# A softplus as small GpSimd operations, and a regrouped fill, in a delta-net mixer

## The chip, the cores and the metric

The kernel runs on one core of one Trainium2 chip. The metric is the device time of one execution in microseconds (us). The engines are named as the profile names them: PE is TensorE's matmul, PEld its weight load, DVE is VectorE, ACT is ScalarE, POOL is GpSimd, SP is SyncE, which here issues DMAs only.

## The reference

Two layers of a decoder trunk on 256 tokens of width 1024, all in float32. Each layer is: half a SwiGLU feed-forward network (FFN), a token mixer, a cross-attention into 256 memory tokens, half an FFN, each on a normalised input and added to x. In layer 0 the mixer is dilated attention beside a gated linear recurrence. In layer 1 it is a gated DeltaNet with 8 heads of 128, the part that the change is about:

```
qkv, z, a, b = split(h @ w_in)                      # 3*1024, 1024, 8, 8 columns
q, k, v = split(silu(causal_dwconv(qkv, conv_w)))   # q, k normalised per head
beta = sigmoid(b)
g = -exp(a_log) * softplus(a + dt_bias)             # log decay, per token and head
o = gated_delta_rule_chunked(q, k, v, g, beta)
o = rmsnorm(o, o_norm) * silu(z)
x = x + o @ w_out
```

The delta rule takes cumulative sums of g, `decay = exp(gcum_i - gcum_j)` below the diagonal, the matrix `I + strict(beta * k k^T * decay)`, a triangular solve with it, and a recurrence over chunks. Layer 0 has a second, smaller softplus: that of `-lam`, for the recurrence.

## The kernel before, in words

**Layout and weights.** Activations stand transposed, features on the 128 partitions and the 256 tokens along the free dimension. A weight block of 1024 rows and 256 columns is a unit. It comes from memory in halves (`raw`), and each half is split into a high part (ACT, L158) and a low part (DVE, L159), `wt`. A product is then a 512-column matmul (L200) and a 256-column one (L204), a pair. A unit has 16 pairs and yields four times. After every yield comes `tick`, which splits the next half of a weight and runs what is due: `self.after(n, fn)` puts a step n ticks ahead.

**The delta-net mixer (`mixer1`).** It first projects the 128 columns that hold a and b. Then `DN_ORDER` gives four parts. The first is nine units (k0 k1 q0 q1 k2 v0 k3 v1 z0; each covers two heads). The second is `back` for the head pairs 0 and 1 with the units after the bar (v3 z1 v2 q2) as fill between its steps. The third is the unit q3 alone. The fourth is `back` for the pairs 2 and 3 with z2 z3 K2 K3 as fill (K are keys of the cross-attention). Each projected unit goes from PSUM (`psw`, three buffers) through an add on ACT and DVE (L270, L271), a convolution (L1071, L1074) and a SiLU.

**The decays.** `AB` sets when, in ticks after the a/b projection, `betas`, `decays`, `decay_rows` and the four loads of e are due. `betas` transposes a and b (L1032), adds the bias (`ga`, L1035), runs `softplus` (L742 to L752, which calls `log1p_of`, a series in z = e / (e + 2)), and multiplies by -exp(a_log) to get g (L1039). `decays` sums g with two matmuls (L1044, L1045). `decay_rows` transposes the sums and writes them to DRAM through ACT's DMA queue (`gd`, L1058). `decay` copies a mask into e on SP's queue and has GpSimd's queue load `gd` onto it, adding (L1119); ACT takes the exponential (L1125) at the ticks of `EXP`. With e, `matrix` (at `NK`) makes `na` (L1169), which is stored, inverted in blocks of 16 on DVE (L1233, L1235) and loaded again as `tu`. `KST`, `QST` and `VST` hold the ticks of the other steps of keys, queries and values.

**The end of a group.** `back` squares and sums o (L1327), takes a power -1/2 on GpSimd (L341, `ro`), and `gated` multiplies o by it and by silu(z) (L1339). `gated_T` transposes the result (L1348) and writes the input of the output projection, a2, as a high part (ACT, L1349) and a low part (DVE, L1350). For pairs 0 and 1 both are due a few ticks into the unit q3. For pairs 2 and 3 they stand at the end of the part, and the output projection follows. `DN_FILL` holds how many yields of fill come after each step of `back`, then ahead of each `gated_T`; what is left comes last.

**What sets the order.** The program is written in this order, but the framework's planner makes one list of instructions for each engine ahead of the run, by its own estimate of when each input is ready, and may move an instruction past others. On the chip each engine runs its list in order.

```
DN_FILL = ((1, 1, 1, 1, 1, 1, 1, 1, 1, 2, 2, 1), (1, 1, 1, 1, 1, 1, 1, 1, 1, 1, 1, 0, 5, 0))
AB = (3, 5, 8, 10, 11, 12, 12)
```

Of the kernel before, what the change touches and what calls it, by code (L numbers as in the profile page):

```python
# [9 lines left out]
F32 = mybir.dt.float32  # L10
# [4 lines left out]
OP = mybir.AluOpType  # L15
# [3 lines left out]
P = 128  # L19
# [6 lines left out]
NEG = -1e30  # L26

DN_ORDER = ('k0 k1 q0 q1 k2 v0 k3 v1 z0', '01|v3 z1 v2 q2', 'q3', '23|z2 z3 K2 K3')
DN_FILL = ((1, 1, 1, 1, 1, 1, 1, 1, 1, 2, 2, 1), (1, 1, 1, 1, 1, 1, 1, 1, 1, 1, 1, 0, 5, 0))
YB = 5  # L30
EB, QB, VB = (4, 3, 3)
TWICE = 'k0 k1 q0 q1'.split()
MASK = 2
EXP = (16, 17, 22, 23)
KST = (0, 7, 3)
QST = (2, 9, 5)
VST = 10
AB = (3, 5, 8, 10, 11, 12, 12)
NK = (13, 10, 10, 9)
INV = (3, 4, 13, 14)  # L40
NST = 1
COVER = (3, 1)
# [5 lines left out]
LN_TERMS = 8  # L48
# [19 lines left out]
class Net:  # L68
# [363 lines left out]
    def setup(self, ctx):  # L432
        nc, tc, t = self.nc, self.tc, self.t
# [8 lines left out]
        c = self.p_c  # L442
# [7 lines left out]
        nc.vector.memset(self.ones, 1.0)  # L450
        self.mhalf = c.tile([P, 32], F32, name="mhalf")
        nc.vector.memset(self.mhalf, -0.5)
        self.prm = c.tile([P, P], F32, name="prm")
        self.dcw = c.tile([P, P], F32, name="dcw")

# [4 lines left out]
        x = t["x"][0].rearrange("(t p) d -> p t d", p=P)  # L460
# [263 lines left out]

    def log1p_of(self, pool, e, n, name):

        nc = self.nc
        z = pool.tile([P, n], F32, name=name + "z")
        y = pool.tile([P, n], F32, name=name + "y")
        s = pool.tile([P, n], F32, name=name + "s")  # L730
        nc.vector.tensor_scalar(z, e, 2.0, None, op0=OP.add)
        nc.vector.reciprocal(z, z)
        nc.vector.tensor_mul(z, z, e)
        nc.vector.tensor_mul(y, z, z)
        nc.vector.tensor_scalar(s, y, 2.0 / (2 * LN_TERMS + 1), None, op0=OP.mult)
        for i in range(LN_TERMS - 1, 0, -1):
            nc.vector.scalar_tensor_tensor(s, s, 2.0 / (2 * i + 1), y, op0=OP.add, op1=OP.mult)
        nc.vector.scalar_tensor_tensor(s, s, 2.0, z, op0=OP.add, op1=OP.mult)
        return s

    def softplus(self, pool, x, n, name, sign=1.0):

        nc = self.nc
        m = pool.tile([P, n], F32, name=name + "m")
        e = pool.tile([P, n], F32, name=name + "e")
        nc.vector.tensor_scalar(m, x, sign, 0.0, op0=OP.mult, op1=OP.max)
        nc.vector.tensor_scalar(e, x, -1.0, None, op0=OP.mult)
        nc.vector.tensor_tensor(e, e, x, op=OP.min)
        nc.scalar.activation(e, e, AF.Exp)
        s = self.log1p_of(pool, e, n, name)  # L750
        nc.vector.tensor_add(s, s, m)
        return s  # L752

    def attn_consts(self, mp, tmp):
# [246 lines left out]
    def mixer1(self, mid, kT_mem, mem_mov, gnext):  # L1001
        nc, tc, t = self.nc, self.tc, self.t
# [3 lines left out]
        with tc.tile_pool(name="m1", bufs=1, reuse_waits="tile") as mp:  # L1006
# [9 lines left out]
            for ks in (range(4), range(4, 8)):  # L1016
# [6 lines left out]
            beta, nbeta, ga, g, gc, ngc, kd, eg, nb_all, hb_all, rq_all, ro_all = map(small, (  # L1023
                "beta", "nbeta", "ga", "g_dn", "gc", "ngc", "kd", "eg", "nb_all", "hb_all", "rq_all", "ro_all"))
# [4 lines left out]
            def betas():  # L1029
                pt = self.bank("s")  # L1030
                for c in range(2):
                    nc.tensor.transpose(pt[:, 0, tok(c)], ab[:, tok(c)], self.ident)  # L1032
                av = pt[:, 0].rearrange("p (c n) -> p c n", c=2)[:, :, 112:120]
                bv = pt[:, 0].rearrange("p (c n) -> p c n", c=2)[:, :, 120:128]
                nc.vector.tensor_add(ga, av, dtb[:, None, :].to_broadcast([P, 2, 8]))  # L1035
                nc.scalar.activation(beta, bv, AF.Tanh, scale=0.5)
                nc.vector.tensor_scalar(nbeta, beta, -0.5, -0.5, op0=OP.mult, op1=OP.add)
                gs = self.softplus(mp, flat(ga), 16, "dt")
                nc.vector.tensor_mul(g, gs.rearrange("p (a b) -> p a b", a=2),  # L1039
                                     nea[:, None, :].to_broadcast([P, 2, 8]))  # L1040

            def decays():
# [52 lines left out]
            def square(y):  # L1095
                sq = mp.tile([P, 2, S], F32, name="th", bufs=2)
                nc.scalar.activation(sq, y, AF.Square)
                return sq
# [12 lines left out]
            def decay(p, n):  # L1111

                e = four("e", EB)

                def mask():
                    nc.sync.dma_start(e, neg_up[:, None, :].to_broadcast([P, 4, P]))

                def load():
                    nc.gpsimd.dma_start(e, bass.AP(tensor=gd.tensor, offset=gd.offset + 4 * p * P,  # L1119
                                                   ap=[[0, P], [1, 4 * P]]), accum_op=OP.add)  # L1120

                def exp():
                    for j in range(2):
                        for c in range(2):
                            nc.scalar.activation(e[:, 2 * j + c], e[:, 2 * j + c], AF.Exp,  # L1125
                                                 bias=ngc[:, c, 2 * p + j:2 * p + j + 1])
                    st[p]["e"] = e

                self.after(MASK, mask)
                self.after(n, load)  # L1130
                self.after(EXP[p], exp)

# [3 lines left out]
            def key_steps(p, y, n, twice):  # L1136
# [40 lines left out]

                k0, k1, k2 = KST
                self.after(k0, lambda: s.update(sq=square(y)))
# [154 lines left out]
            def gated(p):  # L1334
                o, z = st[p]["o"], st[p].pop("z")
                for j in range(2):
                    for c in range(2):
                        i = 2 * j + c
                        nc.vector.scalar_tensor_tensor(o[:, i], o[:, i], ro_all[:, c, 2 * p + j:2 * p + j + 1],  # L1339
                                                       z[:, c, j * P:j * P + P], op0=OP.mult, op1=OP.mult)  # L1340

            def gated_T(p):
                o = st[p].pop("o")
                hs = slice(2 * p, 2 * p + 2)
                po = self.bank("s")
                for j in range(2):
                    for c in range(2):
                        nc.tensor.transpose(po[:, j, tok(c)], o[:, 2 * j + c], self.ident)  # L1348
                nc.scalar.activation(a2[:, hs, 0], po, AF.Copy, scale=onorm)  # L1349
                nc.vector.scalar_tensor_tensor(a2[:, hs, 1], po, onorm, a2[:, hs, 0].bitcast(F32),  # L1350
                                               op0=OP.mult, op1=OP.subtract)
# [3 lines left out]
            def unit(step):  # L1355
# [16 lines left out]
                if kind == "k":  # L1372
                    yks[c] = y
                    key_steps(c, y, NK[c], twice)
                elif kind == "q":
# [3 lines left out]

            assert AB[0] < AB[1] < AB[2] < min(AB[3:]) and max(AB[3:]) < min(EXP)  # L1380
            self.after(AB[0], betas)
            self.after(AB[1], decays)
            self.after(AB[2], decay_rows)
            for p in range(4):
                decay(p, AB[3 + p])
            for i, part in enumerate(DN_ORDER):
                if i % 2 == 0:
                    for step in part.split():
                        self.run(unit(step))
                    continue  # L1390
                group, bg = part.split("|")
                gens = [back(int(p)) for p in group]
                bg = deque(unit(step) for step in bg.split())
                parts = list(DN_FILL[i // 2])
                if i == 1:
                    self.fill(bg, 2)
                while gens:
                    gens = [g_ for g_ in gens if next(g_, 0) is None]
                    if gens:
                        self.fill(bg, parts.pop(0))  # L1400
                if i == 1:
                    self.fill(bg)
                    for n, p in enumerate(group):
                        self.after(1 + n, lambda p=int(p): gated(p))
                        self.after(4 + n, lambda p=int(p): gated_T(p))
                    continue
                for p in group:
                    gated(int(p))
                for p in group:
                    self.fill(bg, parts.pop(0))  # L1410
                    gated_T(int(p))
                self.fill(bg)
# [64 lines left out]
```

## Time and profile before

| | |
|---|---|
| median of three runs | 1252.36 us (1251.72 to 1255.6) |
| the profiled execution | 1251.99 us, its span 1250.2 us |
| granted clock of PE | 0.998 of full speed |
| busy: PE, PEld | 1236.0 us (99%), 1104.9 us (88%) |
| busy: DVE, ACT, POOL | 929.0 us (74%), 752.0 us (60%), 80.5 us (6%) |
| the delta-net mixer in the trace | from 770 us to some 973 us of the span |

The matmuls are pipelined and their ends are modelled, so a busy PE can hide short gaps. A row of the timeline gives the start, the duration, the engine, the line, the operation, output<-input with their shapes, and the count. A bracket at its end holds the idle time of that engine before it and what ended it. A row of waits names who waited, for whom, how long in total, how often, and the longest. A row of a group ends with the busy time, the mean duration in ns, and the idle time before.

### The profile page before, as it was taken

What the parts mean: (1) busy time and instruction counts of PE and PEld (TensorE: products, weight loads), DVE (VectorE), ACT (ScalarE), POOL (GpSimd) and SP (SyncE); (2) the same over time, 40 slices, a digit from 0 to 9 for tenths busy, and PEclk for the clock granted to TensorE, in tenths of its full rate; (3) what the DMA queues carried; (4) which work ended last, traced back from release to release, by engine and by line L of the source; (5) the groups of instructions that cost most, each with busy time, mean ns of one, the idle gap of its engine ahead of it and who ended that gap; (6) DMA issues with size and microseconds to landing.
All of it is one profiled execution on the core that took longest, in us unless ns stands there. A gap on an engine that the chain in (4) does not pass through costs nothing.

```text
span 1250.2 us, 20300 instructions
## 1 busy us (share of the span) xinstructions
PE 1236.0 (99%) x7702; PEld 1104.9 (88%) x7702; DVE 929.0 (74%) x1590; ACT 752.0 (60%) x1281; POOL 80.5 (6%) x96
## 2 busy tenths in 40 slices
PE   9999999999999999999999999999999999999997
PEld 8888889888998888888888888888898998888887
DVE  6987957788668778766877756989757668777753
ACT  7766545886555665545656544776757465666543
POOL 1000020000101000011000001020001101000000
PEclk9999999999999999999999999999999999999999
DMA  8766676544544566557666566667534535666561
GB/s 272 215 206 197 185 255 185 178 125 152 185 135 154 185 198 184 183 185 231 187 187 195 181 192 204 183 153 193 142 99 135 181 124 169 185 186 194 177 194 60
DMA packets 231019, 222.92 MB, mean 178 GB/s; under 512 B 14969, under 2 KB 228617, under 8 KB 230793
## 3 DMA queue, kind: packets, MB, share of 16 engines
q1 hardware_dynamic: 229448, 217.94, 56.9%
q0 software_dynamic: 1152, 3.15, 1.0%
q8 instruction: 60, 0.98, 0.3%
q10 hardware_dynamic: 320, 0.53, 0.1%
q14 instruction: 39, 0.31, 0.1%
HBM read 215.03 MB, written 5.51 MB: 176 GB/s over the span
## 4 chain that ended last, share of the span: by engine, by line
PE 90%; DVE 5%; ACT 2%; DMA 1%; issue 1%; POOL 1%; ACTq 0%; DVEq 0%; POOLq 0%
PE psw L200 21%; PE pss L200 16%; PE psw L204 11%; PE psf L200 11%; PE pss L204 8%; PE psf L204 5%; PE psw L242 5%; PE psf L242 4%; PE pss L242 3%; PE psw L216 2%; DVE wt L159 1%; PE psw L220 1%; ACT wt L158 1%; PE pss L1268 1%; PE psf L1274 1%
## 5 line engine op out<-in xcount | busy, mean ns | idle before, releaser
L159 DVE TENSOR_TENSOR wt<-raw,wt 128x1024 fp32r<-128x1024 f32 (+1 forms) x409 | 484.9, 1191 | 202.8 <-ACT wt L158 199.6
L158 ACT ACTIVATE wt<-raw 128x1024 fp32r<-128x1024 f32 (+1 forms) x409 | 418.6, 1031 | 172.1 <-PE psw L204 59.4
L200 PE MATMUL psw<-x,wt 128*128 128x512 f32 x864 | 310.6, 396 | 2.1 <-DVE xn L271 1.8
L204 PE MATMUL psw<-x,wt 128*128 128x256 f32 x864 | 224.9, 281 | 0.5 <-DVE wt L159 0.5
L200 PE MATMUL pss<-x,wt 128*128 128x512 f32 x520 | 187.4, 393 | 0.0
L200 PEld LDWEIGHTS psw<-x,wt 128*128 128x128 f32 x864 | 160.6, 188 | 30.1 <-issue 2.1
L204 PEld LDWEIGHTS psw<-x,wt 128*128 128x128 f32 x864 | 162.4, 188 | 9.4 <-DVE wt L159 1.0
L204 PE MATMUL pss<-x,wt 128*128 128x256 f32 x520 | 134.9, 280 | 0.0
L200 PE MATMUL psf<-x,wt 128*128 128x512 f32 x352 | 127.2, 394 | 0.0
L200 PEld LDWEIGHTS pss<-x,wt 128*128 128x128 f32 x520 | 97.7, 188 | 16.9 <-ACT bc L377 0.4
L204 PEld LDWEIGHTS pss<-x,wt 128*128 128x128 f32 x520 | 97.7, 188 | 5.4
L200 PE MATMUL psw<-h,wt 128*128 128x512 f32 x264 | 94.9, 396 | 0.0
L204 PE MATMUL psf<-x,wt 128*128 128x256 f32 x352 | 91.3, 280 | 0.0
L200 PE MATMUL pss<-h,wt 128*128 128x512 f32 x242 | 87.0, 396 | 0.0
L336 POOL TENSOR_TENSOR acc<-acc,sq 128x256 f32<-128x256 f32 x49 | 43.7, 891 | 658.3 <-ACT sq L334 557.3
L200 PEld LDWEIGHTS psf<-x,wt 128*128 128x128 f32 x352 | 66.1, 188 | 11.2
L204 PE MATMUL psw<-h,wt 128*128 128x256 f32 x264 | 72.0, 280 | 0.0
L204 PEld LDWEIGHTS psf<-x,wt 128*128 128x128 f32 x352 | 66.2, 188 | 3.5
L204 PE MATMUL pss<-h,wt 128*128 128x256 f32 x242 | 66.0, 280 | 0.0
L200 PEld LDWEIGHTS psw<-h,wt 128*128 128x128 f32 x264 | 49.6, 188 | 10.8
L200 PE MATMUL psf<-h,wt 128*128 128x512 f32 x154 | 55.4, 397 | 0.0
L200 PEld LDWEIGHTS pss<-h,wt 128*128 128x128 f32 x242 | 45.5, 188 | 9.8
(377 smaller groups left out, 2109.2 us busy)
## 6 DMA issues: line engine op xcount, KB each, us to landing
raw<-in_ffn_w_in_dram SPq DMA_DIRECT2D x175, 512.0 KB, 3.6
raw<-in_ffn_w_out_dram SPq DMA_DIRECT2D x80, 512.0 KB, 3.6
raw<-in_xa_wkv_dram SPq DMA_DIRECT2D x32, 512.0 KB, 3.5
raw<-in_dn_w_in_dram SPq DMA_DIRECT2D x32, 512.0 KB, 4.6
raw<-in_ab_w_in_dram SPq DMA_DIRECT2D x20, 512.0 KB, 3.6
raw<-in_xa_wq_dram SPq DMA_DIRECT2D x16, 512.0 KB, 3.5
raw<-in_xa_wo_dram SPq DMA_DIRECT2D x16, 512.0 KB, 3.4
raw<-in_ffn_w_out_dram SPq DMA_DIRECT2D x16, 256.0 KB, 2.9
```

Source lines behind the costliest of these rows:

```text
L158: nc.scalar.activation(a, r, AF.Copy)
L159: nc.vector.tensor_sub(b, r, a.bitcast(F32))
L200: nc.tensor.matmul(out.rearrange("p a s -> p (a s)"), w[:, 0, cols], mov[:, k].rearrange("p a s -> p (a s)"), start=k == start, stop=k == ...
L204: nc.tensor.matmul(out[:, 0], w[:, 1, cols], mov[:, k, 0], start=False, stop=False)
L216: nc.tensor.matmul(out.rearrange("p a s -> p (a s)"), mov[:, k, 0, tok], w.rearrange("p a s -> p (a s)"), start=k == 0, stop=k == KD - 1)
L220: nc.tensor.matmul(out[:, 0], mov[:, k, 1, tok], w[:, 0], start=False, stop=False)
L242: self.nc.tensor.matmul(out, a[u], b[w], start=first and i == 0, stop=last and i == 2)
L336: (eng or nc.gpsimd).tensor_add(self.acc, self.acc, sq)
L1268: nc.tensor.matmul(py[:, i], na[:, i], tu[:, 0, i], start=True, stop=True)
L1274: nc.tensor.matmul(pp[:, i], yy[:, i], tu[:, 1, i], start=True, stop=True)
```

## The change

The softplus runs on GpSimd instead of VectorE, in both places where it is used; only its exponential stays on ACT. It is written with other operations: the minimum of x and -x as -2 max(x, 0) + x, the reciprocal as a power -1 against a constant tile `mone`, and each step of the series as a multiplication and an addition instead of one fused operation. Before the exponential three operations stand as before; after it, the multiplication by -exp(a_log) included, there are 22 instead of 15. The series has the same terms.

The multiplication that gives g moves to GpSimd as well. The tables AB, KST, NK and EXP shift the steps of the decays and keys. For the head pairs 0 and 1 `gated` comes at ticks 2 and 3 instead of 1 and 2, `gated_T` at 6 and 7 instead of 4 and 5. The second group's fill has 9 yields between the steps of `back` instead of 11, 4 ahead of the first `gated_T` instead of 5, and 3 left for after the second one instead of none.

```diff
-DN_FILL = ((1, 1, 1, 1, 1, 1, 1, 1, 1, 2, 2, 1), (1, 1, 1, 1, 1, 1, 1, 1, 1, 1, 1, 0, 5, 0))
+DN_FILL = ((1, 1, 1, 1, 1, 1, 1, 1, 1, 2, 2, 1), (1, 0, 1, 1, 0, 1, 1, 1, 1, 1, 1, 0, 4, 0))
-EXP = (16, 17, 22, 23)
-KST = (0, 7, 3)
+EXP = (16, 18, 22, 23)
+KST = (0, 7, 5)
-AB = (3, 5, 8, 10, 11, 12, 12)
-NK = (13, 10, 10, 9)
+AB = (2, 7, 9, 10, 10, 11, 11)
+NK = (13, 11, 10, 9)
@@ setup
         nc.vector.memset(self.mhalf, -0.5)
+        self.mone = c.tile([P, 32], F32, name="mone")
+        nc.vector.memset(self.mone, -1.0)
@@ log1p_of
-        nc.vector.tensor_scalar(z, e, 2.0, None, op0=OP.add)
-        nc.vector.reciprocal(z, z)
-        nc.vector.tensor_mul(z, z, e)
-        nc.vector.tensor_mul(y, z, z)
-        nc.vector.tensor_scalar(s, y, 2.0 / (2 * LN_TERMS + 1), None, op0=OP.mult)
-        for i in range(LN_TERMS - 1, 0, -1):
-            nc.vector.scalar_tensor_tensor(s, s, 2.0 / (2 * i + 1), y, op0=OP.add, op1=OP.mult)
-        nc.vector.scalar_tensor_tensor(s, s, 2.0, z, op0=OP.add, op1=OP.mult)
+        eng.tensor_scalar(z, e, 2.0, None, op0=OP.add)
+        eng.tensor_tensor(z, z, self.mone[:, :n], op=OP.pow)
+        eng.tensor_mul(z, z, e)
+        eng.tensor_mul(y, z, z)
+        eng.tensor_scalar(s, y, 2.0 / (2 * LN_TERMS + 1), 2.0 / (2 * LN_TERMS - 1), op0=OP.mult, op1=OP.add)
+        for i in range(LN_TERMS - 2, -1, -1):
+            eng.tensor_mul(s, s, y)
+            eng.tensor_scalar(s, s, 2.0 / (2 * i + 1), None, op0=OP.add)
+        eng.tensor_mul(s, s, z)
@@ softplus
-        nc.vector.tensor_scalar(m, x, sign, 0.0, op0=OP.mult, op1=OP.max)
-        nc.vector.tensor_scalar(e, x, -1.0, None, op0=OP.mult)
-        nc.vector.tensor_tensor(e, e, x, op=OP.min)
+        eng.tensor_scalar(m, x, sign, 0.0, op0=OP.mult, op1=OP.max)
+        eng.tensor_scalar(e, m, -2.0, None, op0=OP.mult)
+        (eng.tensor_add if sign > 0 else eng.tensor_sub)(e, e, x)
         nc.scalar.activation(e, e, AF.Exp)
         s = self.log1p_of(pool, e, n, name)
-        nc.vector.tensor_add(s, s, m)
+        eng.tensor_add(s, s, m)
@@ mixer1
-                nc.vector.tensor_mul(g, gs.rearrange("p (a b) -> p a b", a=2),
+                nc.gpsimd.tensor_mul(g, gs.rearrange("p (a b) -> p a b", a=2),
-                        self.after(1 + n, lambda p=int(p): gated(p))
-                        self.after(4 + n, lambda p=int(p): gated_T(p))
+                        self.after(2 + n, lambda p=int(p): gated(p))
+                        self.after(6 + n, lambda p=int(p): gated_T(p))
```

More of the change, by code (lines that the diff above doesn't have):

```diff
@@ L725, in log1p_of @@
     def log1p_of(self, pool, e, n, name):
-        nc = self.nc
+        eng = self.nc.gpsimd
         z = pool.tile([P, n], F32, name=name + "z")
@@ L743, in softplus @@
         nc = self.nc
+        eng = nc.gpsimd
         m = pool.tile([P, n], F32, name=name + "m")
         e = pool.tile([P, n], F32, name=name + "e")
-        nc.vector.tensor_scalar(m, x, sign, 0.0, op0=OP.mult, op1=OP.max)
-        nc.vector.tensor_scalar(e, x, -1.0, None, op0=OP.mult)
-        nc.vector.tensor_tensor(e, e, x, op=OP.min)
+        eng.tensor_scalar(m, x, sign, 0.0, op0=OP.mult, op1=OP.max)
+        eng.tensor_scalar(e, m, -2.0, None, op0=OP.mult)
+        (eng.tensor_add if sign > 0 else eng.tensor_sub)(e, e, x)
         nc.scalar.activation(e, e, AF.Exp)
         s = self.log1p_of(pool, e, n, name)
-        nc.vector.tensor_add(s, s, m)
+        eng.tensor_add(s, s, m)
         return s
```

## The prediction

> **What bounds the kernel now.** I read the page first, then the waits of TensorE (PE), then stretches of the delta-net mixer.
>
> ```profile
> span 1250.2 us, 20300 instructions
> ...
> PE 1236.0 (99%) x7702; PEld 1104.9 (88%) x7702; DVE 929.0 (74%) x1590; ACT 752.0 (60%) x1281; POOL 80.5 (6%) x96
> ```
>
> PE sets the end: 14.2 us of the span are not PE work, and nothing in the diff takes work from PE. A gain can only come out of stalls of PE. The waits of PE, longest first (total, times, longest, in us):
>
> ```profile
> PE psw L200 <- DVE xn L271: 1.8, 1, 1.8
> PE psf L200 <- DVE a L1350: 1.3, 1, 1.3
> PE psw L491 <- DVE mhalf L452: 1.1, 1, 1.1
> PE pss L1348 <- DVE qk L1339: 1.0, 1, 1.0
> ...
> PE psw L216 <- DVE tm L1233: 0.4, 1, 0.4
> ```
>
> All but the third lie in the delta-net mixer, so at most 1.8 + 1.3 + 1.0 + 0.4 = 4.5 us can be had there: 0.36% of the run. A measurement of this kernel can tell about 0.3% from no change, which is 3.8 us. The two windows around the first stall (length, then PE, PEld, DVE, ACT, POOL busy):
>
> ```profile
> 790.00:800.00 10.00, 10.00 (x62) 8.76 (x60) 9.96 (x28) 9.02 (x16) 0.00 (x0) 1.00 0.78 216
> ...
> 810.00:820.00 10.00, 8.78 (x60) 7.78 (x58) 6.72 (x18) 5.89 (x16) 5.46 (x6) 1.00 0.72 134
> ```
>
> While the softplus runs, PE is full and VectorE (DVE) is full with it. In the window with the stall every engine has room: something is waited for in a chain. That chain is this:
>
> ```profile
> 791.14 0.16 DVE L1035 TENSOR_TENSOR ga<-pss,dtb 128x16 f32<-128x16 f32 x1
> ...
> 805.39 0.17 DVE L1039 TENSOR_TENSOR g_dn<-dts,alog 128x16 f32<-128x16 f32 x1
> ```
> ```profile
> 808.64 2.12 DMA gd<-gt
> ...
> 811.35 6.14 DMA e<-gd
> ```
> ```profile
> 794.40 1.28 ACT L749 ACT_TABLE_LOAD   x1
> 795.70 0.22 ACT L749 ACTIVATE dte<-dte 128x16 f32<-128x16 f32 x1
> ...
> 817.51 0.99 ACT L1125 ACTIVATE e<-e,ngc 128x128 f32<-128x128 f32 x3 [3.95 <-DMA e<-gd]
> ```
>
> The decays g are ready at 805.6; their rows go out (2.1 us), come back as e (6.1 us), and ScalarE (ACT) stands 3.95 us at 817.5 for e. The evictions of the projection stand behind that exponential on ACT and behind L1169 on DVE, so PE runs out of psw banks and waits its 1.8 us. If g comes earlier, this stall shrinks by as much, down to zero.
>
> **The order of PE is set before the run.** A tick is four pairs of matmuls:
>
> ```profile
> 792.29 0.39 PE L200 MATMUL psw<-x,wt 128*128 128x512 f32 x1
> ...
> 793.68 0.39 PE L200 MATMUL psw<-x,wt 128*128 128x512 f32 x1
> ```
> ```profile
> 789.97 0.38 PE L1032 MATMUL pss<-ident,xn 128*128 128x128 f32 x2
> ...
> 805.62 0.39 PE L1044 MATMUL pss<-g_dn,dn_triu 128*128 128x16 f32 x2
> ```
>
> Four pairs take 793.68 - 792.29 = 1.39 us. The tables of before put betas (L1032) and decays (L1044) two ticks, 2.8 us, apart; on the chip they are 15.65 us, 11 ticks, apart, with projection matmuls between. So the planner moves work to where it thinks the input is ready, and here it judged VectorE's chain right: L1044 starts 0.06 us after g. The tables are earliest times only.
>
> **Part 1, the softplus of the decays.** It takes 18 operations off DVE: three before the exponential and 15 after, g included. The groups of DVE in 790 to 806 us (busy, mean ns, idle before):
>
> ```profile
> L159 DVE TENSOR_TENSOR wt<-raw,wt 128x1024 fp32r<-128x1024 f32 x7 | 8.6, 1222 | 0.6 <-ACT wt L158 0.5
> L1074 DVE SCALAR_TENSOR_TENSOR y<-xn,dcw,y 128x255 f32<-128x255 f32 (+2 forms) x12 | 5.7, 471 | 0.0
> L271 DVE TENSOR_TENSOR xn<-psw,xn 128x256 f32<-128x256 f32 x5 | 2.1, 418 | 0.0
> L737 DVE SCALAR_TENSOR_TENSOR dts<-dts,dty 128x16 f32<-128x16 f32 x7 | 1.2, 169 | 0.0
> ```
>
> At 0.17 us each that is 18 x 0.17 = 3.1 us of DVE, about half of it hidden in the overlap of neighbours. PE is full there, so this is worth nothing by itself; it lets DVE reach the stall with a shorter queue.
>
> It adds 25 operations on GpSimd (POOL): three, then the exponential, then 21 small ones and one power of 16 elements in place of the reciprocal. No row shows a small arithmetic operation of POOL; the nearest ones:
>
> ```profile
> 145.54 0.24 POOL L969 IOTA mem<- 128x128 int32 x1 [43.69 <-DVE mem L769]
> ```
> ```profile
> L336 POOL TENSOR_TENSOR acc<-acc,sq 128x256 f32<-128x256 f32 x49 | 43.7, 891 | 658.3 <-ACT sq L334 557.3 <-DMA raw<-in_xa_wkv_dram 100.7
> ```
> ```profile
> 407.76 0.70 POOL L341 TENSOR_TENSOR rcol<-ms,mhalf 128x2 f32<-128x2 f32 x1 [2.68 <-DVE ms L366]
> ...
> 841.13 1.01 POOL L341 TENSOR_TENSOR rs_dn<-ss,mhalf 128x4 f32<-128x4 f32 x1 [5.77 <-DVE ti L1235]
> ```
> ```profile
> 331.91 1.23 DVE L159 TENSOR_TENSOR wt<-raw,wt 128x1024 fp32r<-128x1024 f32 x1
> ...
> 332.02 1.68 POOL L341 TENSOR_TENSOR rcol<-ms,mhalf 128x2 f32<-128x2 f32 x1 [9.29 <-DVE ms L366]
> ```
>
> A power of 2 elements takes 0.70 us and one of 4 takes 1.01, so 0.155 us an element; for 16 elements I estimate 0.39 + 16 x 0.155 = 2.9 us (1.0 if it does not grow further). A small operation lies between the iota's 0.24 and the 0.89 of an add sixteen times as wide; 16 elements are nearest to the iota, so 0.25. But the last pair of rows shows a price on top: the power that met a running L159 took 1.68 instead of 0.70, and ended 0.6 us after L159 did. POOL waits for the DVE operation with two SBUF inputs that runs. In 790 to 806 L159 and L1074 alone are 14.3 of 16 us, and the 25 DVE operations that remain (7 + 12 + 5 and one L1081) are 0.64 us apart. If every POOL operation waits for one of them, it costs 0.64.
>
> The Trainium skill states the rule behind that row: in "SBUF — State Buffer", section "Who interferes with whom", a DVE instruction with two SBUF inputs and a GpSimd instruction that reads SBUF exclude each other for the whole instruction. The pair of rows agrees.
>
> So from ga to g, with 1.5 us for table load and exponential: at best 24 x 0.25 + 2.9 + 1.5 = 10.4 us, at worst 24 x 0.64 + 2.9 + 1.5 = 19.8. Some operations fall beside L271, which reads PSUM, or into gaps; I take 0.45, which gives 10.8 + 2.9 + 1.5 = 15.2 us. Before it was 805.56 - 791.14 = 14.4. AB[0] goes from 3 to 2, so ga starts one tick (1.39 us) earlier. g then lands at 791.14 - 1.39 + 15.2 = 805.0, half a microsecond earlier: **-0.5** (between the full -1.8 and, at worst, a g of 809.6, 4 us late). The other way round, POOL could hold up DVE:
>
> ```profile
> 841.45 0.20 DVE L1233 TENSOR_TENSOR tm<-nb,ti 64x64 f32<-64x64 f32 x1
> ```
>
> This one, with two SBUF inputs, ran beside the power of 841.13 to 842.14 and took its usual 0.20, so I take nothing (24 x 0.25 = 6 us of DVE time, some 2 us more than its gaps, if each operation locked it out whole).
>
> New waits: the exponential on ACT now waits for POOL's first three operations, and behind it stand evictions of psw (L270); DVE's L807 (nsp, in the first FFN) waits for the chain of lam, and behind it stand the splits of the weights (L159). Both are waits of a microsecond or so if the planner has the chain too short, with PE full and weights and banks ahead of it: nothing, or up to 1 us each without that cover. PE's own new wait, L1044 for POOL, is the rival below. The other shifted tables (AB, KST, NK, EXP) move work by one or two ticks within the projection, and POOL's four loads of e come after the softplus as before. The memset of "mone" goes ahead of PE's 1.1 us wait on L452 and lengthens it by at most 0.1, before any weight or x has come: nothing.
>
> **Part 2, the gated rows of heads 0 to 3.**
>
> ```profile
> 902.43 0.33 PE L1348 MATMUL pss<-ident,qk 128*128 128x128 f32 x1 [1.00 <-DVE qk L1339]
> ```
>
> L1348 stands 1.0 us for L1339, which stands for the power ro. The transposes move from tick 4 to tick 6, so 2 x 1.39 = 2.8 us more of projection or fill stand before them. That covers the 1.0: **-1.0** (0 if the planner pulls them forward again). What is late next is a2 of these heads, which nobody reads before the output projection.
>
> **Part 3, the fill of the second group.**
>
> ```profile
> 930.41 0.73 DVE L1275 COPY_PREDICATED tu<-dn_m,psf 128x512 f32<-128x512 uint8 x1
> ```
> ```profile
> 939.62 0.48 PE L200 MATMUL psw<-m,wt 128*128 128x512 f32 x1
> ...
> 940.15 1.83 PE L1317 MATMUL pss<-vb,qk 128*128 128x128 f32 x14
> ...
> 948.43 1.03 PE L1348 MATMUL pss<-ident,qk 128*128 128x128 f32 x8
> ...
> 953.60 0.50 PE L200 MATMUL psf<-a,wt 128*128 128x512 f32 x1 [1.34 <-DVE a L1350]
> ```
>
> The 16 ticks of fill (z2, z3, K2, K3) were 11 between the steps of back and 5 before the transposes L1348; now they are 9 and 4, and 3 are left behind the transposes. Before, the output projection followed L1348 at once and stood 1.34 us for the low part of its input, L1350. Three ticks, 4.2 us, now lie between: this stall goes, -1.3. Against it, two steps lose their fill, both behind the masked copy L1275: 0.73 us each, 1.5 in all, if nothing else is put there. But the planner does put work there: at 939.62 it slipped a pair of the fill between the products L1317, where the table has a 0. I charge 0.3. The one tick less before L1348 is covered by the same three ticks, if the planner moves them. Together **-1.0** (-1.3 to +0.2).
>
> **Sum.** -0.5 - 1.0 - 1.0 = -2.5 us. The profiled execution took 1251.99 us, 1.79 more than its span; its span less 2.5 is 1247.7, its time 1249.5. The runs before have a median of 1252.36, 0.4 above the profiled one, and reach from 1251.72 to 1255.6, so the forecast, **1249.5**, is 0.2% below the median: hardly to be told from no change.
>
> **Rivals.**
>
> A, PE stands for the decays: slower. The planner places L1044 from its own price of POOL. Nothing shows that it counts the slow power or the waits for DVE's reads; on DVE it had only operations that it knows well. The earliest place is tick 7: betas at tick 3 were at 789.97, and four ticks of 1.39 later is 795.5. With g at 805.0, PE would stand up to 9.5 us. It would be less, since a standing PE gives DVE nothing to evict, and POOL then runs at 0.25: of the 24 x 0.2 = 4.8 us that the waits cost, perhaps a third falls away. That leaves 8 us; the stall at 820, up to 1.8, is absorbed in it, and parts 2 and 3 still give 2.0: +8 - 1.8 - 2.0 = +4.2, 1256.2. It decides from the point where g comes 3.8 us after L1044's place; below that it only eats the gain. For it: all PE stalls now left lie behind POOL, a DMA or a long DVE queue. Against it: tick 7 is five ticks (7 us) after betas instead of two, and the best case of the chain is 10.4 us.
>
> B, all stalls of the mixer go: faster. If few operations of POOL meet DVE, g comes at 791.14 - 1.39 + 10.4 = 800.2, more than the 1.8 us earlier that the stall needs; with DVE's shorter queue the 0.4 at L1233 goes too: -1.8 - 0.4 - 1.0 - 1.3 = -4.5, 1247.5. For it: POOL has nothing else to do then. Against it: DVE's 9.96 of 10.
>
> C, the change does not do what it says: the tables are earliest times, and the planner already fills. The stalls L1348 and L1350 are misjudged waits that only move, and g comes when it did: 0 to -1, 1251.5.
>
> The Trainium skill would speak for A: "GPSIMD Engine Reference", section "Engine selection", puts elementwise work with two inputs on VectorE, GpSimd being about twice as slow. No run here shows that ratio for operations this small.
>
> **How the numbers follow.** Forecast 0.34, B 0.27, C 0.19, A 0.20. Faster by over 0.3% (below 1248.6): B, and 0.10 from the better end of the forecast (-3.8 needs 1.3 us more than its sum), 0.37. Slower (above 1256.1): 0.14 of A's 0.20, since POOL holding up DVE, or the waits on ACT and L807, would come on top of its price; 0.49 is left within. The range takes B, with up to 2 us more should DVE's relief reach further, and A up to a stall of about 7 us: 1245.5 to 1255.5. Below it are 0.05, above it 0.15.
>
> **What would show it.** In the profile after: g on POOL at about 805 and L1044 on PE without a wait (A: a wait of PE for POOL g there, several us); POOL's small operations 0.25 to 0.64 us apart, and the power of 16 elements near 2.9 us; PE's wait on DVE xn L271 below 1.8; no wait of PE for qk L1339 or a L1350; a filled PE around L1275. The prediction is wrong if PE stalls at a place that the page before does not show, or if the three stalls stand where they stood.

## The result and the profile after

The changed kernel takes 1262.82 us (median of six runs, 1261.02 to 1263.37) against 1252.41 us for the kernel before in the same comparison (six runs, 1251.72 to 1256.03). The ratio of the runs is 1.0072, with an interval of 1.0059 to 1.0084: slower by 0.7%, and above the predicted range, which ended at 1255.5. (The two medians by themselves are 0.8% apart.) The profiled execution took 1261.02 us, the shortest of the six and 9.0 us more than that of before; its span is 8.8 us longer. Lines of the mixer now have numbers four higher: L1044 is L1048, L1348 is L1352, L1039 is L1043 and so on.

The page of the kernel after:

```profile
span 1259.0 us, 20320 instructions
...
PE 1239.5 (98%) x7702; PEld 1106.4 (88%) x7702; DVE 925.7 (74%) x1556; ACT 753.5 (60%) x1283; POOL 99.8 (8%) x145
```

The operations moved as the diff says (DVE has 34 fewer, POOL 49 more), and PE has the same 7702 matmuls. The waits of PE, kernel after (total, times, longest, in us):

```profile
PE pss L1048 <- POOL g_dn L1043: 7.1, 1, 7.1
PE pss L1272 <- DMA tu<-d: 1.6, 2, 0.9
...
PE psf L1278 <- issue: 0.7, 1, 0.7
...
PE psf L1278 <- DVE qk L1203: 0.4, 1, 0.4
PE pss L1352 <- DVE qk L1343: 0.4, 1, 0.4
...
PE psw L216 <- DVE ti L1239: 0.2, 1, 0.2
```

None of the 1.8, 1.3 and 1.0 us waits of before is left. The first row is new and larger than all of them together: PE stands 7.1 us for g from POOL. It is rival A. The stretches around it (length, then PE, PEld, DVE, ACT, POOL busy with their counts, then granted clock, DMA share, GB/s), two of before first:

```profile
800.00:805.00 5.00, 5.00 (x31) 4.37 (x30) 4.92 (x17) 2.98 (x5) 0.00 (x0) 1.00 0.68 199
805.00:810.00 5.00, 5.00 (x35) 4.39 (x34) 4.56 (x18) 3.47 (x9) 0.64 (x1) 1.00 0.80 214
```

and three of the kernel after:

```profile
795.00:800.00 5.00, 1.55 (x9) 1.10 (x7) 2.35 (x4) 2.17 (x5) 4.24 (x10) 0.92 0.65 199
800.00:805.00 5.00, 1.33 (x6) 1.33 (x7) 0.26 (x2) 0.05 (x1) 2.69 (x12) 0.50 0.01 3
805.00:810.00 5.00, 5.00 (x19) 4.20 (x19) 3.80 (x10) 2.72 (x6) 0.00 (x0) 0.55 0.26 54
```

From 800 until PE's restart at 803.67 only POOL works. In 805 to 810 PE is full again by its busy time, but does 19 matmuls instead of 35: the granted clock is 0.55. The loss is 0.45 x 5 = 2.25 us there and half of the 1.3 us from PE's restart at 803.67 to 805, so about 2.9 us by the granted clock. Then the balance of the span closes. New waits 7.1 + 1.6 + 0.7 + 0.4 + 0.4 + 0.2 = 10.4; the four waits of before that went, 1.8 + 1.3 + 1.0 + 0.4 = 4.5; the clock 2.9: +10.4 - 4.5 + 2.9 = +8.8, as measured. (The experiment on the clock puts it at 2.4 to 2.6, which leaves some 0.4 us without a name.) The page's own totals split much the same way: PE stands 1259.0 - 1239.5 = 19.5 us instead of 14.2, 5.3 more, and is busy 3.5 us longer with the same matmuls.

Why PE comes to stand is seen in what lies between the transposes for the betas and the matmuls for the decays. The groups of PE's operations in that stretch, before and after:

```profile
L200 PE MATMUL psw<-x,wt 128*128 128x512 f32 x43 | 14.9, 397 | 0.0
```
```profile
L200 PE MATMUL psw<-x,wt 128*128 128x512 f32 x19 | 6.6, 398 | 0.0
```

In the kernel before, the planner put 43 pairs of the projection between them, in the kernel after only 19, which is 19 x 0.348 = 6.6 us of work. So g was expected on PE's list after some 6.6 us. The table `AB` has a share in this place: it puts five ticks, 20 pairs, between betas and decays, and the decays stand about there, at the earliest tick that they may. POOL's chain in the timeline of the kernel after:

```profile
791.78 0.31 POOL L750 TENSOR_SCALAR dtm<-ga 128x16 f32<-128x16 f32 x1 [14.58 <-DVE ga L1039]
792.18 1.03 POOL L751 TENSOR_SCALAR dte<-dtm 128x16 f32<-128x16 f32 x1
...
794.26 3.06 POOL L734 TENSOR_TENSOR dtz<-dtz,mone 128x16 f32<-128x16 f32 x1
797.40 0.22 POOL L735 TENSOR_TENSOR dtz<-dtz,dte 128x16 f32<-128x16 f32 x1
797.70 0.21 POOL L736 TENSOR_TENSOR dty<-dtz 128x16 f32<-128x16 f32 x1
...
803.39 0.22 POOL L1043 TENSOR_TENSOR g_dn<-dts,alog 128x16 f32<-128x16 f32 x1
```

The power takes 3.06 us, the small operations follow each other every 0.3 us or so, and g is ready at 803.61, 11.8 us after the start. More than half of that is with an idle VectorE: DVE, in the timeline of the same kernel, stood from 797.4 on, because the next instruction on its list, L1051, copies what L1049 makes on PE, and PE stood for g.

```profile
791.53 0.16 DVE L1039 TENSOR_TENSOR ga<-pss,dtb 128x16 f32<-128x16 f32 x1
...
804.74 0.17 DVE L1051 COPY gc<-pss 128x16 f32<-128x16 f32 x1 [7.32 <-PE pss L1049]
```

### The profile page after: what moved, and what is told of

It is laid out like the page before. It is cut to its first block, busy times and chain, and to the rows that moved or that the text cites. A ratio compares the mean times of both kernels' runs of the same rounds, so it can differ in the third digit from the quotient of the medians.

```text
span 1259.0 us, 20320 instructions
## 1 busy us (share of the span) xinstructions
PE 1239.5 (98%) x7702; PEld 1106.4 (88%) x7702; DVE 925.7 (74%) x1556; ACT 753.5 (60%) x1283; POOL 99.8 (8%) x145
## 4 chain that ended last, share of the span: by engine, by line
PE 91%; DVE 4%; ACT 2%; POOL 1%; DMA 1%; issue 1%; SPq 0%; ACTq 0%; DVEq 0%; POOLq 0%
PE psw L200 22%; PE pss L200 15%; PE psw L204 11%; PE psf L200 10%; PE pss L204 8%; PE psf L204 5%; PE psw L242 5%; PE psf L242 4%; PE pss L242 3%; DVE wt L159 1%; PE psw L216 1%; PE pss L1272 1%; PE psf L1278 1%; PE psw L220 1%; DMA tu<-d 0%
## 5 line engine op out<-in xcount | busy, mean ns | idle before, releaser
L200 PE MATMUL psw<-x,wt 128*128 128x512 f32 x864 | 313.1, 398 | 0.3 <-DVE x L311 0.2
L200 PE MATMUL pss<-x,wt 128*128 128x512 f32 x520 | 188.0, 394 | 0.0
L200 PEld LDWEIGHTS psw<-x,wt 128*128 128x128 f32 x864 | 161.3, 189 | 28.2 <-DVE x L311 0.8
L204 PEld LDWEIGHTS psw<-x,wt 128*128 128x128 f32 x864 | 163.8, 190 | 10.4 <-DVE wt L159 1.7
L200 PE MATMUL psf<-x,wt 128*128 128x512 f32 x352 | 127.5, 394 | 0.0
L200 PEld LDWEIGHTS pss<-x,wt 128*128 128x128 f32 x520 | 97.6, 188 | 17.1 <-ACT bc L377 0.4
L200 PE MATMUL psw<-h,wt 128*128 128x512 f32 x264 | 94.9, 396 | 0.0
L200 PE MATMUL pss<-h,wt 128*128 128x512 f32 x242 | 87.0, 396 | 0.0
L200 PEld LDWEIGHTS psf<-x,wt 128*128 128x128 f32 x352 | 66.1, 188 | 11.3
L200 PEld LDWEIGHTS psw<-h,wt 128*128 128x128 f32 x264 | 49.6, 188 | 10.8
L200 PE MATMUL psf<-h,wt 128*128 128x512 f32 x154 | 55.4, 397 | 0.0
L200 PEld LDWEIGHTS pss<-h,wt 128*128 128x128 f32 x242 | 45.5, 188 | 9.8
```

The source lines that it names most:

```text
L200: nc.tensor.matmul(out.rearrange("p a s -> p (a s)"), w[:, 0, cols], mov[:, k].rearrange("p a s -> p (a s)"), start=k == start, stop=k == ...
L204: nc.tensor.matmul(out[:, 0], w[:, 1, cols], mov[:, k, 0], start=False, stop=False)
```

## The experiments

**The parts one by one.** First the changed kernel with the softplus and g back on DVE in their old form; tables, gated rows and fill stay as changed.

```diff
@@ log1p_of, softplus: as before the change
-                nc.gpsimd.tensor_mul(g, gs.rearrange("p (a b) -> p a b", a=2),
+                nc.vector.tensor_mul(g, gs.rearrange("p (a b) -> p a b", a=2),
```

> The changed kernel with the softplus and g back on VectorE in the old form; all tables, the gated rows and the fill as changed. The decays stand 41 pairs behind betas. Theory (the softplus alone makes it slower): no wait for g, 1250 to 1252.5. Rival (the shifted tables NK, EXP, KST bring tu later and cost the 2 us that PE waits for it): 1253 to 1256, with PE waiting for tu.

(The constant `mone` is still set, and nothing reads it.) It took 1253.35 us (12 runs), a ratio of 0.9994 (0.9984 to 1.0005): the time of before. No wait for g is left, as the theory had it; the time and the wait for tu are the rival's. Between betas and decays this kernel has 42 pairs on PE's list, with the very `AB` table under which the changed kernel has 19. So the engine of the chain, not the table, decides the place. Its waits of PE (line numbers of the mixer two higher than before):

```profile
PE pss L1270 <- DMA tu<-d: 2.4, 1, 2.4
...
PE psf L1276 <- issue: 0.8, 1, 0.8
...
PE psf L1276 <- DVE qk L1201: 0.4, 1, 0.4
PE pss L1350 <- DVE qk L1341: 0.4, 1, 0.4
```

The three stalls of before have gone, and 2.4 + 0.8 + 0.4 + 0.4 = 4.0 us of other stalls stand in their place.

Then the kernel before with the softplus and g on POOL, nothing else changed:

```diff
@@ log1p_of, softplus: as in the change, with `mone`
-                nc.vector.tensor_mul(g, gs.rearrange("p (a b) -> p a b", a=2),
+                nc.gpsimd.tensor_mul(g, gs.rearrange("p (a b) -> p a b", a=2),
```

> The kernel before with the softplus and g on GpSimd, nothing else changed. The decays stand 17 pairs (5.9 us) behind betas where the chain took 12 us in the changed kernel. Theory: PE waits 6 to 8 us for g, then some us at a lower granted clock; 1260 to 1264. Rival (the new tables place the decays too early): the old tables would give no stall, 1251 to 1254.

It took 1260.43 us (6 runs), 1.0051 (1.0037 to 1.0064). Its waits of PE:

```profile
PE pss L1048 <- POOL g_dn L1043: 7.3, 1, 7.3
PE psf L200 <- DVE a L1354: 1.3, 1, 1.3
...
PE pss L1352 <- DVE qk L1343: 1.0, 1, 1.0
```

That is the theory. The new wait comes with part 1 alone, under the old tables (17 pairs instead of 43). Those tables ask for two ticks, 8 pairs, only; so the 17 are the planner's own, some 5.9 us for a chain that takes 12.3 here. The stall near 820 has gone all the same: g is earlier than before (803.32), and DVE has been emptied by the stall.

Last of these, the kernel before with parts 2 and 3 and nothing on POOL:

```diff
-... (1, 1, 1, 1, 1, 1, 1, 1, 1, 1, 1, 0, 5, 0))
+... (1, 0, 1, 1, 0, 1, 1, 1, 1, 1, 1, 0, 4, 0))
-                        self.after(1 + n, lambda p=int(p): gated(p))
-                        self.after(4 + n, lambda p=int(p): gated_T(p))
+                        self.after(2 + n, lambda p=int(p): gated(p))
+                        self.after(6 + n, lambda p=int(p): gated_T(p))
```

> The kernel before with the later gated rows and the regrouped fill of the second group alone. The prediction's sum for these two is -2.0 us: 1250.4, without PE's waits for qk L1339 (1.0) and a L1350 (1.3). Rival (the stalls only move, or the steps that lost their fill cost as much): 1252 to 1253.

It took 1252.93 us (12 runs), 0.9997 (0.9986 to 1.0008): no difference. Its waits of PE:

```profile
PE psw L200 <- DVE xn L271: 1.9, 1, 1.9
...
PE psf L1274 <- issue: 0.8, 1, 0.8
...
PE psf L1274 <- DVE qk L1199: 0.4, 1, 0.4
...
PE pss L1348 <- DVE qk L1339: 0.4, 1, 0.4
...
PE pss L1280 <- DVE tu L1275: 0.3, 1, 0.3
```

That is the rival's time. The 1.0 us at L1348 and the 1.3 at L1350 are gone; 0.8 and 0.4 at L1274, 0.4 at L1348 and 0.3 at L1280 are new. The work that covers one place was taken from another. To see which part does which, the two were also run alone, one execution each.

> The kernel before with the gated rows of heads 0 to 3 later, alone. The prediction's step: PE's 1.0 us wait for qk L1339 goes. Rival, from the run of both parts: the transposes were the cover of the first step of the second group's inversion, and a wait of 0.8 to 1.0 us at L1274 comes in its place.

```profile
PE psf L200 <- DVE a L1350: 1.3, 1, 1.3
...
PE psf L1274 <- issue: 0.8, 1, 0.8
```

> The kernel before with the regrouped fill of the second group, alone. The prediction's step: PE's 1.3 us wait for a L1350 goes, 0.3 comes. Rival, from the run of both parts: waits of PE at L1274 (0.4) and L1348 (0.4), with the gaps around them about 1.4 us in all, take its place.

```profile
PE pss L1348 <- DVE qk L1339: 1.4, 2, 1.0
...
PE psf L1274 <- DVE qk L1199: 0.4, 1, 0.4
```

The gated rows alone trade the 1.0 at L1348 for 0.8 at L1274. The fill alone ends the 1.3 at L1350 and adds 0.4 at L1348 and 0.4 at L1274. The rest of the 1.3 comes back as well, in gaps too short for the list of waits: from the last transpose of the first group (L1348) to the last L200 of the output projection it takes 965.24 - 905.53 = 59.7 us, and in the kernel before 961.91 - 902.43 = 59.5. These two executions took 1254.54 and 1255.31 us, which by themselves say nothing: the kernel before ran between 1252.63 and 1255.97 beside them. Both had a lower granted clock behind the stall near 820, to which the last section returns.

**Does it help to let PE come later?** The changed kernel with later due times for the decays, so that PE has projection work until g is there:

```diff
-AB = (2, 7, 9, 10, 10, 11, 11)
+AB = (2, 13, 14, 15, 15, 15, 15)
-KST = (0, 7, 5)
+KST = (0, 7, 10)
```

> The changed kernel, with decays due 13 ticks after the a/b projection instead of 7 (AB 2, 13, 14, 15, 15, 15, 15; the keys' rows, which need the decays, 10 ticks after their unit instead of 5). On PE's list the decays then stand 42 pairs behind betas instead of 19, which is 14.6 us instead of 6.6. Theory (PE stands for a softplus that the planner has too short): no wait of PE for g, or under 2 us of it, and the time back at 1250 to 1254. Rival (the softplus on POOL costs by itself, by holding up VectorE or by coming too late for e): still 1257 or more, with stalls elsewhere.

It took 1259.46 us (8 runs), 1.0042 (1.0027 to 1.0056): better than the change, still slower than before, and the rival's time. POOL and DVE in its timeline, two fences:

```profile
791.95 0.17 DVE L1039 TENSOR_TENSOR ga<-pss,dtb 128x16 f32<-128x16 f32 x1
```
```profile
798.12 1.07 POOL L736 TENSOR_TENSOR dty<-dtz 128x16 f32<-128x16 f32 x1
...
800.08 1.11 POOL L740 TENSOR_SCALAR dts<-dts 128x16 f32<-128x16 f32 x1
...
806.39 0.22 POOL L1043 TENSOR_TENSOR g_dn<-dts,alog 128x16 f32<-128x16 f32 x1
```

PE's wait for g is down to 0.3 us, so the order on PE was the cause of the 7.1. But with PE busy, DVE is busy too, and POOL's operations meet it: L736 and the first L740 took 0.21 and 0.26 us in the kernel after and take 1.07 and 1.11 here. From the start of ga to the end of g it is now 806.61 - 791.95 = 14.7 us, against 803.61 - 791.53 = 12.1 in the kernel after. The longer chain alone does not explain the loss, though: g is ready at 806.61, only 1.1 us later than in the kernel before. Two more things come behind it. POOL's next operation, the power for `rs_dn` (L341), has to wait for the end of the chain and starts at 806.57; VectorE's L1150 needs it, and DVE stands 2.6 us, until 807.64. Then DVE works through 3.6 us of other operations on its list and takes the sums of g (L1051) at 811.36, some 4 us after PE made them; in the kernel before it took them at 806.61, 0.4 us after. The rows leave 6 us later than before (814.6 instead of 808.6). How much of this delay comes from the later due times by themselves was not separated. The stalls then lie behind it. Waits of PE and two windows of this kernel:

```profile
PE pss L1272 <- DMA tu<-d: 2.1, 2, 1.2
PE psw L200 <- DVE xn L271: 1.4, 1, 1.4
...
PE pss L1060 <- DVE gch L1052: 1.1, 1, 1.1
...
PE pss L1048 <- POOL g_dn L1043: 0.3, 1, 0.3
```
```profile
830.00:835.00 5.00, 3.85 (x17) 3.36 (x18) 5.00 (x12) 4.98 (x13) 1.26 (x1) 0.76 0.61 164
835.00:840.00 5.00, 5.00 (x21) 4.48 (x22) 4.10 (x12) 3.63 (x7) 1.18 (x1) 0.56 0.82 217
```

The granted clock is at half here for 6.8 us, behind a wait of 1.4 us at 830.5 and one of 0.6 at 831.6. By the granted clock that is 3.4 us of what this kernel loses.

**How much of the wait is the power?** The changed kernel with the power replaced by DVE's reciprocal:

```diff
-        eng.tensor_tensor(z, z, self.mone[:, :n], op=OP.pow)
+        self.nc.vector.reciprocal(z, z)
```

> The changed kernel with the power of -1 (3.06 us on GpSimd) replaced by VectorE's reciprocal (0.24 us before), all else on GpSimd. The decays stand 19 pairs behind betas as in the changed kernel. Theory (PE's wait is the chain's length less the planner's): 2.8 us less, plus some 0.6 for handing over twice: the wait falls from 7.1 to about 4.8, the time to 1259 to 1261. Rival (the number of small operations and their waits for VectorE set it, so that the power's time is made up by waiting): 6.5 or more, 1262 to 1263.

It took 1260.49 us (4 runs), 1.0057 (1.0039 to 1.0075). The wait for g shrank from 7.1 to 5.3 us:

```profile
PE pss L1048 <- POOL g_dn L1043: 5.3, 1, 5.3
```

So with the power replaced the wait is 1.8 us shorter, near the theory. It is less than the 2.8 between the two operations' times, since the hand-overs cost something and one small operation, L737, now meets a split and takes 1.14 us instead of 0.20. The larger part of the wait remains: the chain still takes 10.4 us from ga to g, and PE's list has 19 or 20 pairs, some 7 us of work, for that time.

**How much is the clock?** The changed kernel with 32 matmuls of ones put ahead of the decays' matmuls, into a part of the bank that nothing reads; they are extra work for PE which the result does not need.

```diff
+                for _ in range(32):
+                    nc.tensor.matmul(pgc[:, 1, :P], self.ones, self.ones, start=True, stop=True)
```

> The changed kernel with 32 matmuls of ones by ones put ahead of the two matmuls of decays, into an unused half of their PSUM bank; they add work that no result needs. At 0.24 us each (14 of them took 3.35 us at the start of the run) they fill 7.7 us, about the 7.1 us that PE stood for g. Theory (besides the wait itself, the low granted clock after it costs some 3 us: 0.50 and 0.55 in the two stretches of 5 us from 800): the clock stays at 1.00 and the time falls by 2 to 3 us, to 1260 to 1261, though PE does more. Rival (the clock in the records costs nothing): 1263 or more.

It took 1260.61 us (4 runs), 1.006 (1.0042 to 1.0078). Waits of PE and two windows:

```profile
PE pss L1050 <- POOL g_dn L1043: 1.8, 1, 1.8
```
```profile
800.00:805.00 5.00, 3.20 (x29) 3.01 (x27) 0.73 (x2) 0.94 (x2) 3.80 (x15) 1.00 0.29 99
805.00:810.00 5.00, 4.97 (x31) 4.45 (x32) 2.38 (x7) 2.79 (x7) 0.00 (x0) 1.00 0.00 0
```

With a wait of 1.8 instead of 7.1 the clock stays at 1.00, and 805 to 810 holds 31 matmuls instead of 19. Median against median the gain is 2.2 us, although g comes at 804.98, 1.4 us later than in the kernel after. But the two intervals overlap, and the wait for tu has shrunk as well, from 1.6 to 0.3 us, so the times do not tell what the clock costs. A stretch of PE's list does. From the decays to the next L1107 (L1109 here) PE has the same work in both kernels, but for one matmul more here. It takes 812.55 - 803.67 = 8.9 us in the kernel after and 811.51 - 805.03 = 6.5 us here. So some 2.4 to 2.6 us of the loss is the clock behind the stall, a little under the 2.9 that the granted clock gives.

**What the tables alone can do.** The kernel before with every step of `AB` due one tick earlier, the softplus on DVE:

```diff
-AB = (3, 5, 8, 10, 11, 12, 12)
+AB = (2, 4, 7, 9, 10, 11, 11)
```

> The kernel before, softplus on VectorE, with the steps of the decays one tick earlier: AB 2, 4, 7, 9, 10, 11, 11 instead of 3, 5, 8, 10, 11, 12, 12. On PE's list the decays then stand 6 pairs (2.1 us) nearer the a/b projection. Theory (PE's 1.8 us wait at 820 is e coming late, and its length decides whether the granted clock falls behind it): that wait is gone or under 0.5 us, no stretch behind it below 1.00, and the median 1249 to 1251, 0.2 to 0.3% under the kernel before. Rival (something else is late next, as in the changed kernel, where PE waits for tu): as before, 1252 to 1254.

It took 1251.45 us (12 runs), 0.9987 (0.9975 to 0.9998): a small gain, a little less than was expected. ga starts at 791.02 and g ends at 803.74: 12.7 us, against 14.4 in the kernel before; DVE now takes the first operations of the softplus ahead of a split. The 1.8 us near 820 are gone, but for 0.4; waits of 1.1 for tu and 0.5 at L1274 have come, so that something else is late next, as the rival said.

The kernel before with the change's `AB` and `KST`, and the old `EXP`, `NK`, gated rows and fill (`mone` is set, and nothing reads it):

```diff
-KST = (0, 7, 3)
+KST = (0, 7, 5)
-AB = (3, 5, 8, 10, 11, 12, 12)
+AB = (2, 7, 9, 10, 10, 11, 11)
```

> The kernel before, softplus on VectorE, with the new AB 2, 7, 9, 10, 10, 11, 11 and KST 0, 7, 5, but the old EXP, NK, gated rows and fill. Theory (the shifted EXP and NK of the second key pair, one tick each, brought tu later and made the 2.4 us wait for it in the run with the softplus back on VectorE): the wait for tu is at most 1 us, none at 820, 1249 to 1251. Rival (the wait for tu comes from elsewhere): 2 us of it again, 1252 to 1254.

It took 1251.55 us (12 runs), 0.9984 (0.9971 to 0.9997), just above the 1249 to 1251 that were expected. Its wait of PE for tu:

```profile
PE psf L1276 <- DMA tu<-d: 0.6, 1, 0.6
```

It is 0.6 us where the kernel with all of the change but the softplus has 2.4. Parts 2 and 3 without the tables have no such wait at all. So the difference between 0.6 and 2.4 comes with the later `EXP` and `NK`, by themselves or together with the new gated rows and fill; these were not separated. That PE waits for tu at all is not theirs alone: with the old `EXP` and `NK` and the earlier `AB` it was 1.1 us, and with the new ones and the matmuls of ones it was 0.3.

Last, the earlier `AB` of above with one yield of the second group's fill kept for after the transposes; all eleven between the steps of `back` stay.

```diff
-... (1, 1, 1, 1, 1, 1, 1, 1, 1, 1, 1, 0, 5, 0))
+... (1, 1, 1, 1, 1, 1, 1, 1, 1, 1, 1, 0, 4, 0))
-AB = (3, 5, 8, 10, 11, 12, 12)
+AB = (2, 4, 7, 9, 10, 11, 11)
```

> The run with AB one tick earlier, and one tick of the second group's fill moved from ahead of the last transposes to behind them (4 instead of 5). Theory: a 1.39 us tick covers most of PE's 1.3 us wait for a L1350, and the transposes wait some 0.5 us more: 0.5 to 1 us below the run without it, 1248 to 1250. Rival (the stall only moves, as with the whole regrouping): the same time as the run without it.

It took 1250.87 us (12 runs) beside 1253.04 for the kernel before, 0.9976 (0.9964 to 0.9987), and beats both kernels. By the medians it is 0.6 us under the run without the moved yield, as expected, though their intervals overlap. One tick behind the transposes is enough to end the 1.3 us at L1350. The largest waits of PE in the mixer are now the old 1.0 for the gated rows of heads 0 to 3, with one of 0.5 at the last transposes beside it, and the one for tu:

```profile
PE pss L1348 <- DVE qk L1339: 1.5, 2, 1.0
PE psf L1274 <- DMA tu<-d: 1.3, 1, 1.3
```

Part of what these last three kernels gain goes with the clock. Of the 29 runs of the kernel before beside them, eight have a granted clock of 0.997 or less over the run; of the twelve of each of these kernels none, one and one have. Among the runs at 0.998 or more the means lie 0.8, 1.4 and 1.8 us under the kernel before, where all runs give 1.9, 2.1 and 2.7.

## Why the prediction was wrong, step by step

**The step that failed** is the one on POOL's chain and PE's list: "PE's own new wait, L1044 for POOL, is the rival below", with a chance of 0.20, and in the sum a part 1 of -0.5. Part 1 was +7.1 of wait, and 2.4 to 2.9 of clock behind it. The prediction had seen that the planner moves the decays to where it thinks g is ready, and that nothing shows it to know POOL's costs. It then treated the good place that VectorE's chain has as a sign that POOL's would be good as well. The runs show the contrary: 42 or 43 pairs for a chain on DVE, 17 to 19 for the chain on POOL, under the tables of before and of the change, while the chip needs 12.7 to 14.4 us for the first and 12.1 to 14.7 for the second.

**Rival A** had the mechanism right: PE stopped at about 796.5 (tick 7 had been put at 795.5), DVE ran empty, POOL ran uncontended, and the stall near 820 was absorbed. Its price of 8 us less 1.8 came near 7.1 less 1.8. Its total of +4.2 was too low against +8.8 for three reasons: the clock, 2.9 by the granted clock, which no part of the prediction had; a late tu, 1.6; and parts 2 and 3, credited with 2.0, where 2.3 us of waits went and 0.7 + 0.4 + 0.4 came. Those are 2.9 + 1.6 + 1.2 = 5.7 us, less 0.9 by which the wait was shorter than priced and 0.2 at the head of the inversion.

**Terms of the sum, by the runs.** The power of 16 elements, estimated at 2.9, took 3.06. A small POOL operation, estimated at 0.25 uncontended, took 0.20 to 0.27, though 0.30 from start to start. With a busy DVE the worst case was taken as 0.64; single operations behind a split took 1.03 to 1.11, but most took less, and the chain came to 14.7 against the estimated 15.2. The credit of 1.39 for the earlier betas failed: the transposes for them come 0.3 us earlier (789.66 instead of 789.97), and ga starts at 791.53 instead of 791.14, in its place in DVE's order. That lam's chain, `mone` and ACT's exponential would cost nothing fits the waits: none of PE names them. That POOL would not hold up DVE holds for the kernel after; with the later due times DVE did stand 2.6 us for POOL, though for an operation queued behind the softplus and not for a locked port. The tables, costed at nothing, came with a wait for tu of 1.6 us here and 2.4 with the softplus on DVE; how much of it is `EXP` and `NK` is open.

**Parts 2 and 3**, forecast at -1.0 each, measured 0.9997 together. The waits named did go, and the working for each was right as far as it went. What was missing is where the cover came from: 0.3 us was charged for the fill taken from `back`, and nothing for what the transposes had covered at L1274, their old place, where 0.8 us opened when they alone were moved. Rival C, that these stalls "only move", is what happened there.

**Rival B** is out: the old stalls did all go, as it said, but the time went to others. For the profile's signs the prediction gave the right test: "a wait of PE for POOL g there, several us".

The prediction weighed "GPSIMD Engine Reference", section "Engine selection", of the Trainium skill as a rule in favour of A. The runs now have its ratio for small operations with two inputs: 0.21 to 0.27 us against 0.17, so less than the factor of two that the page gives. The factor is far larger for the one operation without a counterpart, 3.06 us for the power against 0.25 for DVE's reciprocal.

## What to carry to other kernels

Where a planner fixes each engine's order ahead of the run, a chain moved to another engine is priced anew, and an error of that price is paid by the in-order engine that waits for it; look at how much work the planner leaves between the chain's start and its first reader, and compare it with the chain's real length. An engine that looks idle is not free while its operations wait for another engine's: here the moved chain was no faster under load (14.7 us) than it had been on a busy VectorE (12.7 to 14.4), and the operation queued behind it on GpSimd made VectorE stand 2.6 us. A wait of a microsecond that is covered with work taken from nearby comes back there, so run such a part alone before crediting it.

## What the runs showed of the hardware that was not expected

**A stall of PE costs more than its length.** After the wait of 7.1 us the granted clock was 0.50 until 809.5, for 5.8 us of PE's work, worth 2.9 us by the granted clock. It also fell after shorter waits: after 1.4 and 0.6 us with the later due times (above), after 2.3 us with the gated rows alone and after 2.0 us with the fill alone (windows of the last two kernels):

```profile
820.00:825.00 5.00, 3.11 (x11) 2.75 (x11) 4.44 (x13) 5.00 (x13) 0.00 (x0) 0.66 0.97 236
```
```profile
820.00:825.00 5.00, 4.43 (x23) 4.29 (x23) 4.69 (x14) 5.00 (x11) 0.00 (x0) 0.71 0.79 198
```

It did not fall after waits of 1.8 us (before), 1.9 (parts 2 and 3 together) or 2.4 (the kernel with the softplus on DVE):

```profile
860.00:865.00 5.00, 2.62 (x18) 2.02 (x17) 4.29 (x8) 1.00 (x3) 0.00 (x0) 1.00 1.00 268
```

So the length of a wait alone does not decide. The Trainium skill, "TensorE: Matmul & The Clock Gate", Part 1, has the clock halved after an idle window of about 3.4 us that runs freely of the kernel, and warns of idle gaps longer than that. Short windows of these traces, 0.1 us each, agree with the window. Apart from those in which it changes, the clock in them is either 1.00 or 0.50, and a time at 0.50 in the mixer lasts 3.42 us (gated rows alone), 6.82 or 6.83 (fill alone, later due times, softplus alone, reciprocal on DVE) or 10.24 (the kernel after): one, two or three times 3.413. The clock falls once more at the end of every run, and that fall lies on the same grid: in the kernel after it is at 1256.62, which is 447.15 us, 131 times 3.413, behind the rise at 809.47. So the end of a run tells where the stretches of 3.413 us lie in it, also where the clock did not fall before.

Counted in these stretches, the waits sort themselves. In the stretch ahead of each of the six falls in the mixer PE was busy for 1.50 us or less: 0.73 in the kernel after, 1.45 with the later due times, 1.40 with the gated rows alone, 1.50 with the fill alone, none in the other two. Where the clock did not fall, the emptiest stretch of the mixer had more. With the softplus on DVE it had 1.60 us, since a border cuts the wait of 2.4 into 1.8 and 0.6; with parts 2 and 3 together it had 1.82; in the kernel before it had 2.20, the wait of 1.8 being cut into 0.6 and 1.2. So, other than by the page's rule, PE need not be idle for a whole window: a stall of some 2 us is enough if it falls into one stretch, and the same stall does no harm to the clock if a border halves it. The limit is not sharp. Near the end of three runs (gated rows alone, tables alone, the last kernel above) stretches with 1.48 to 1.51 us brought no fall. Why the clock comes back after one, two or three stretches stays open.

The spread of the kernel before goes with the clock. Of its 25 runs in one comparison, the nine from 1255.14 to 1256.6 us have a granted clock of 0.996 or 0.997 over the run, and the sixteen from 1251.72 to 1254.83 have 0.998 or 0.999. That the clock falls behind the 1.8 us stall in those nine is likely, but not shown, since there is no trace of them.

**POOL's operations wait for VectorE's even where they read one tensor only.** L751, 1.03 us in the kernel after, and L740, 1.11 in the one with later due times, have one tensor as input and otherwise take 0.2 to 0.4 us. The operation that L751 met is this one on DVE, in the kernel after; L751 ended 0.11 us behind it:

```profile
791.87 1.23 DVE L159 TENSOR_TENSOR wt<-raw,wt 128x1024 fp32r<-128x1024 f32 x1 [0.17 <-ACT wt L158]
```

The prediction charged such waits to every small operation, from a row of a two-input power; these rows show them for one input.
